# Hybrid encoder on one core: the gate z projected 512 columns at a time, and a place of its own for each final half's 1/rms

## The chip, the cores and the metric

The kernel runs on one core of a Trainium2 chip. The metric is the device time of the whole program in microseconds; smaller is better. Before the change it is 1213.37 us, the median of three runs (1212.6 to 1213.63).

The core's engines run side by side, each through its own instructions in a fixed order, and wait for each other through semaphores: TensorE (PE; its weight loads are listed as PEld), VectorE (DVE), ScalarE (ACT), GpSimd (POOL), and SyncE (SP), which here only issues transfers between HBM and the on-chip memory. Matrix products land in PSUM banks, each of 128 partitions by 512 float32.

## What is computed

Two layers of a hybrid encoder over 512 tokens of width 1024, float32, then a final RMSNorm. Cut to what matters here:

```python
for i in range(DEPTH):                                   # DEPTH = 2
    h = rms_norm(x, norm_mix_w[i])
    proj = jnp.einsum("bld,de->ble", h, w_in[i])
    q, k, v, z, xbc_raw, dt_raw = jnp.split(proj, split_at, axis=-1)   # z: 512 columns
    ...                                                  # attention on q, k, v
    ssd_out = ssd_mixer(z, xbc_raw, dt_raw, ...)         # scan in 4 chunks of 128 tokens
    x = x + jnp.einsum("ble,ed->bld", jnp.concatenate([attn_out, ssd_out], -1), w_out[i])
    x = x + ffn(rms_norm(x, norm_ffn_w[i]))              # SwiGLU
return rms_norm(x, final_norm_w)

# at the end of ssd_mixer
y = y.reshape(b, l, SSD_WIDTH) * jax.nn.silu(z)          # the gate
yg = y.reshape(b, l, SSD_GROUPS, SSD_WIDTH // SSD_GROUPS)
yg = yg * lax.rsqrt(jnp.mean(yg * yg, axis=-1, keepdims=True) + EPS)
```

## The kernel before, in words

Activations lie transposed: 8 tiles of 128 features by 512 tokens. Every float32 operand of a large product is split into a rounded high part and a low rest, and a product is three matmuls, high by high, high by low and low by high (`mm3` L417, `mm3a` L423).

**The weight stream.** All weights come in pieces of 128 by 1024 in one fixed list, `chunks` (L109 to L133): per layer k/v/dt, then what `ORDER` (L54) names (x for the convolved x/B/C columns, q and z in two halves of 256 columns of two pieces each), then eight pieces of w_out, then the FFN. SP loads a piece into one of two raw buffers (`load` L169, bufs=2). ACT casts it to the high part and DVE subtracts to the low part, 512 columns at a time (L191, L192), into one of four buffers each (WB, L31). `next` (L196) splits the piece asked for and the two after it (`AHEAD = 2`) and loads a third.

**The mixer** (L446 to L977) interleaves three generators (`drain` L892): `att` (32 heads-by-query-blocks, four per block: scores L712/L713, maximum on DVE L714, exponential on ACT L716, transposes L719, product with V L729), `fill` (the projections of `ORDER`, and after the scan the first half of the output product, `out_half` L824) and `ssd` (decay matrices L759 to L798, `chunk` L800 with L804 and L812, `finish` L917). This order of emission is a priority; a list scheduler then fixes each engine's final order. In `token_major` (L431) the stationary operand is a 128 by 128 block of tokens and the moving one a weight block of 256 columns: for one half of z, 4 token chunks of 8 row blocks of 3 matmuls (L427, L428, L429). `z_done` (L850) empties a chunk's bank: tanh and a scaled copy on ACT (L856, L857), one combining instruction on DVE (L858).

**The end.** `Last` (L361) turns the last FFN product's tiles back to token rows. The last tile comes in two halves of 256 tokens (`down` L382): each half's mean of squares becomes 1/rms by an integer guess and three Newton steps on DVE (`rsqrt` L285, twelve instructions behind L400), and two 128-row blocks are scaled by it (on ACT L407 and L410, on DVE L412) and sent out in four transfers (L413). `rsqrt` keeps its result in a place named after its argument `name` (L288), one buffer deep.

Of the kernel before, what the change touches and what calls it, by code (L numbers as in the profile page):

```python
# [15 lines left out]
F32 = mybir.dt.float32  # L16
F32R = mybir.dt.float32r
I32 = mybir.dt.int32
AF = mybir.ActivationFunctionType
# [4 lines left out]
P = 128  # L24
# [3 lines left out]
S = 512  # L28
# [25 lines left out]
ORDER = "x4 q0 x5 x7 x6 x3 x0 x1 x2 q1 z0 z1".split()  # L54
# [24 lines left out]
def tile_hybrid_encoder(ctx, tc, xt_d, par_d, rope_d, snw_d, w_kvdt, w_xbc, w_q, w_z, w_out, w_gate, w_up, w_down, out_d):  # L79
# [29 lines left out]
    for l in range(L):  # L109
# [3 lines left out]
        for what in ORDER:  # L113
            i, lo = int(what[1]), what in POOL_LO
            if what[0] == "x":
                stream(w_xbc[l, i], 1024, lo, 512)
            else:
                for j in range(2):
                    stream({"q": w_q, "z": w_z}[what[0]][l, 2 * i + j], 1024, lo, 512)
# [15 lines left out]
    class Stream:  # L135
# [40 lines left out]
        def fetch(self, j, a, b, queue=nc.sync):  # L176
            self.fetched[j] = queue.dma_start(self.raw[j][:, a:b], chunks[j][0][:, a:b])
# [183 lines left out]
    class Last(Norm):  # L361
# [20 lines left out]
        def down(self, m, cols):  # L382
# [18 lines left out]
            rt = rsqrt(nrm, mm, 2, "rfin")  # L401
# [29 lines left out]
    def token_major(ps, op, n, after=None, behind=None):  # L431

        w = W.take(2)
        for c in range(NC):
            b = ps[c] if isinstance(ps, list) else ps(c)
            for k in range(KT):
                wh, wl = (t[:, k % 4 * n:(k % 4 + 1) * n] for t in w[k // 4])
                with tc.issue_after(behind.ins) if behind and c == 0 and k > 1 else nullcontext():
                    mm3a(b[:, :n], wh, wl, op, k, c, k == 0, k == KT - 1)
            if after is not None:  # L440
                after(c, b)
            yield

    nrm0 = Norm(pc("nmix", 0, 8), xT)

    def mixer(l, norm, mx):  # L446
# [403 lines left out]
        def z_done(hf):  # L850
            def fin(c, ps):
                if hf not in gz:
                    gz[hf] = mx.tile([P, NC, 256], F32, name=f"gz{hf}", tag=("kd", "Btok")[hf])
                th = mx.tile([P, 256], F32, name="zth", tag="t3", bufs=B3)
                zs = gz[hf][:, c]
                A.activation(th, ps[:, :256], AF.Tanh, scale=rth[:, c:c + 1])  # L856
                A.activation(zs, ps[:, :256], AF.Copy, scale=rth[:, c:c + 1])  # L857
                V.scalar_tensor_tensor(zs, th, 1.0, zs, ALU.add, ALU.mult)  # L858
            return fin

        def fill():
            for what in ORDER:
                i = int(what[1])
                if what[0] == "q":
                    yield from qproj(i)
                elif what[0] == "z":
                    yield from token_major(lambda c: bank("a"), op, 256, z_done(i))
# [338 lines left out]
```

## Time and profile before

| | us |
|---|---|
| median of three runs | 1213.37 |
| the profiled execution | 1212.78 |
| its span, first to last instruction | 1211.0 |
| PE busy | 1190.3 (98%) |
| DVE busy | 902.2 (75%) |
| ACT busy | 633.3 (52%) |
| POOL busy | 149.8 (12%) |

PE is busy in nearly every slice and its granted clock stands at the top level nearly throughout. The span holds, for each of two layers, a mixer (about 20 to 260 us and 600 to 850 us) and an FFN, and at the end the output of the final norm, in which PE no longer works. Busy shares are means over these stretches: what an edit is worth is read in its own stretch.

### The profile page before, as it was taken

The page shows a single profiled execution, that of the slowest core. Times are in us where ns is not written, and L with a number is a line of the kernel's source. Part 1 is how long each engine was busy: PE and PEld are TensorE (multiplying, and loading weights), DVE is VectorE, ACT ScalarE, POOL GpSimd, SP SyncE. Part 2 cuts the span into 40 slices and gives each one's busy share as a digit, 9 for nine tenths or more (in the row PEclk, how much of TensorE's full clock was granted, in tenths as well). Part 3 has the DMA queues.
Part 4 walks back from the last instruction along what each step waited for, and adds up shares of the span by engine and source line. Part 5 has one row for each costly group of instructions (what it writes and reads, how often), then busy time and mean ns, then how long its engine had stood idle before and what let it go on. Part 6 is the DMA issues. An engine that isn't in the chain of part 4 may idle for free.

```text
span 1211.0 us, 19732 instructions
## 1 busy us (share of the span) xinstructions
PE 1190.3 (98%) x7720; PEld 1056.5 (87%) x7720; DVE 902.2 (75%) x1477; ACT 633.3 (52%) x1208; POOL 149.8 (12%) x140
## 2 busy tenths in 40 slices
PE   9999999999999999999999999999999999999996
PEld 7889887788899899899898888878879989989985
DVE  7999986568886676677779977866688857847842
ACT  5668775344444354254556876844335524533634
POOL 0202432012000000000211053401020000000011
PEclk9999999999999999999999999999999999999998
DMA  6221111225143233231433111312242432332121
GB/s 223 96 75 54 44 53 53 73 84 165 58 135 123 70 122 114 67 100 40 151 126 103 60 35 56 95 33 91 81 146 96 140 105 70 124 108 83 36 79 70
DMA packets 47534, 110.04 MB, mean 91 GB/s; under 512 B 5425, under 2 KB 5937, under 8 KB 47441
## 3 DMA queue, kind: packets, MB, share of 16 engines
q1 hardware_dynamic: 46720, 107.68, 28.0%
q8 instruction: 60, 0.98, 0.3%
q10 hardware_dynamic: 720, 1.11, 0.3%
q14 instruction: 34, 0.27, 0.1%
HBM read 104.44 MB, written 4.33 MB: 90 GB/s over the span
## 4 chain that ended last, share of the span: by engine, by line
PE 89%; DVE 5%; ACT 3%; DMA 1%; issue 1%; POOL 0%; SPq 0%; ACTq 0%; DVEq 0%; POOLq 0%
PE ps_a L1068 6%; PE ps_a L1067 6%; PE ps_a L1066 6%; PE ps_a L419 5%; PE ps_a L420 5%; PE ps_a L421 5%; PE ps_s L1112 3%; PE ps_s L1114 3%; PE ps_s L1113 3%; PE ps_a L1113 3%; PE ps_a L1112 3%; PE ps_a L1114 3%; PE ps_s L1068 3%; PE ps_s L1067 3%; PE ps_s L1066 3%; PE ps_t L729 3%
## 5 line engine op out<-in xcount | busy, mean ns | idle before, releaser
L191 ACT CAST whi<-wraw 128x512 fp32r<-128x512 f32 (+4 forms) x183 | 125.5, 714 | 211.6 <-PE ps_a L420 52.7
L191 ACT CAST whi<-sraw 128x1024 fp32r<-128x1024 f32 x126 | 131.7, 1050 | 141.0 <-DVE sraw L166 40.4
L192 DVE TENSOR_TENSOR wlo<-wraw,whi 128x512 fp32r<-128x512 f32 (+4 forms) x183 | 149.4, 831 | 54.2 <-ACT whi L191 53.1
L192 DVE TENSOR_TENSOR wlo<-sraw,whi 128x1024 fp32r<-128x1024 f32 x126 | 153.6, 1223 | 46.3 <-ACT whi L191 46.1
L328 POOL TENSOR_TENSOR ssq<-ssq,sqt 128x512 f32<-128x512 f32 x17 | 24.9, 1463 | 680.0 <-ACT sqt L325 679.3
L419 PE MATMUL ps_a<-xh,whi 128*128 128x512 f32 x272 | 107.2, 397 | 0.6 <-DVE x L834 0.3
L421 PE MATMUL ps_a<-xh,wlo 128*128 128x512 f32 x272 | 106.6, 392 | 0.0
L420 PE MATMUL ps_a<-xl,whi 128*128 128x512 f32 x272 | 106.3, 392 | 0.0
L166 DVE TENSOR_TENSOR sraw<-sraw 128x1024 f32<-128x1024 f32 x72 | 88.0, 1222 | 1.0
L1068 PE MATMUL ps_a<-ss,wlo 128*128 128x256 f32 x288 | 81.7, 284 | 0.0
L1066 PE MATMUL ps_a<-ss,whi 128*128 128x256 f32 x288 | 81.5, 283 | 0.0
L1067 PE MATMUL ps_a<-ss,whi 128*128 128x256 f32 x288 | 81.5, 283 | 0.0
L1068 PE MATMUL ps_a<-s,wlo 128*128 128x256 f32 x288 | 81.1, 283 | 0.0
L1067 PE MATMUL ps_a<-s,whi 128*128 128x256 f32 x288 | 81.1, 283 | 0.0
L1066 PE MATMUL ps_a<-s,whi 128*128 128x256 f32 x288 | 79.8, 283 | 0.0
L427 PE MATMUL ps_a<-whi,xh 128*128 128x256 f32 (+1 forms) x256 | 74.2, 291 | 0.1
L428 PE MATMUL ps_a<-wlo,xh 128*128 128x256 f32 (+1 forms) x256 | 73.9, 290 | 0.0
L429 PE MATMUL ps_a<-whi,xl 128*128 128x256 f32 (+1 forms) x256 | 71.9, 286 | 0.0
L1113 PE MATMUL ps_a<-hid,whi 128*128 128x512 f32 x176 | 68.9, 391 | 1.7 <-DVE hid L1012 1.7
L1112 PE MATMUL ps_s<-hid,whi 128*128 128x512 f32 (+1 forms) x182 | 70.0, 385 | 0.3 <-DVE a__3261 L1009 0.2
L1113 PE MATMUL ps_s<-hid,whi 128*128 128x512 f32 (+1 forms) x182 | 69.8, 384 | 0.0
L1114 PE MATMUL ps_s<-hid,wlo 128*128 128x512 f32 (+1 forms) x182 | 69.7, 383 | 0.0
(412 smaller groups left out, 3441.7 us busy)
## 6 DMA issues: line engine op xcount, KB each, us to landing
sraw<-in_w_gate SPq DMA_DIRECT2D x72, 256.0 KB, 3.3
sraw<-in_w_up SPq DMA_DIRECT2D x72, 256.0 KB, 4.0
wraw<-in_w_down SPq DMA_DIRECT2D x48, 384.0 KB, 3.2
wraw<-in_w_xbc SPq DMA_DIRECT2D x16, 512.0 KB, 3.2
wraw<-in_w_out SPq DMA_DIRECT2D x16, 512.0 KB, 3.3
wraw<-in_w_q SPq DMA_DIRECT2D x8, 512.0 KB, 3.5
wraw<-in_w_z SPq DMA_DIRECT2D x8, 512.0 KB, 3.3
wraw<-in_w_gate SPq DMA_DIRECT2D x8, 512.0 KB, 3.2
```

The source lines that it names most:

```text
L166: V.tensor_tensor(q[to], q[to], q[by], ALU.add)
L191: A.copy(hi[:, u], raw[:, u])
L192: (G if lo_pool else V).tensor_tensor(lo[:, u], raw[:, u], hi[:, u].bitcast(F32), ALU.subtract)
L419: T.matmul(ps, lhsT=wh, rhs=op.h[k], start=first, stop=False)
L420: T.matmul(ps, lhsT=wh, rhs=op.l[k], start=False, stop=False)
L421: T.matmul(ps, lhsT=wl, rhs=op.h[k], start=False, stop=last)
L1066: T.matmul(out, lhsT=wh[:, o:o + P], rhs=x_[:, 0, i], start=first and i + j == 0, stop=False, skip_group_check=True)
L1067: T.matmul(out, lhsT=wh[:, o:o + P], rhs=x_[:, 1, i], start=False, stop=False, skip_group_check=True)
L1068: T.matmul(out, lhsT=wl[:, o:o + P], rhs=x_[:, 0, i], start=False, stop=i == 3, skip_group_check=True)
L1112: T.matmul(ps[:, cols], lhsT=w1[:, o:o + P], rhs=h, start=f == a, stop=False)
L1113: T.matmul(ps[:, cols], lhsT=w1[:, o:o + P], rhs=g, start=False, stop=False)
L1114: T.matmul(ps[:, cols], lhsT=w2[:, o:o + P], rhs=h, start=False, stop=f == b - 1)
```

## The change

Two edits that have nothing to do with each other.

The final halves' 1/rms get a name each (`rfin0`, `rfin1`), so that each has its own buffer.

z is projected in one pass of 512 columns instead of two of 256. Its four weight pieces, which held four row blocks of 256 columns, now hold two row blocks of 512 columns; as the arrays in HBM are as before, each piece is loaded by two transfers, one for each half of the columns. All four pieces are needed for every token chunk, so `token_major` takes four pieces before the first chunk, and with `AHEAD = 0` it splits nothing beyond them. One bank of 512 columns is emptied by one tanh of 512 columns, two copies of 256 and two combining instructions of 256. The generator yields twice per chunk, so that its eight turns in `drain` stay.

```diff
-ORDER = "x4 q0 x5 x7 x6 x3 x0 x1 x2 q1 z0 z1".split()
+ORDER = "x4 q0 x5 x7 x6 x3 x0 x1 x2 q1 z".split()
...
         for what in ORDER:
-            i, lo = int(what[1]), what in POOL_LO
+            i, lo = int(what[1:] or 0), what in POOL_LO
             if what[0] == "x":
                 stream(w_xbc[l, i], 1024, lo, 512)
             else:
-                for j in range(2):
-                    stream({"q": w_q, "z": w_z}[what[0]][l, 2 * i + j], 1024, lo, 512)
+                for j in range(2 if what[0] == "q" else 4):
+                    if what[0] == "q":
+                        stream(w_q[l, 2 * i + j], 1024, lo, 512)
+                    else:
+                        u = slice(j % 2 * 512, j % 2 * 512 + 512)
+                        stream([w_z[l, h + j // 2][:, u] for h in (0, 2)], 1024, lo, 512)
...
         def fetch(self, j, a, b, queue=nc.sync):
-            self.fetched[j] = queue.dma_start(self.raw[j][:, a:b], chunks[j][0][:, a:b])
+            src = chunks[j][0]
+            if isinstance(src, list):
+                for i, s in enumerate(src):
+                    to = self.raw[j].rearrange("p (k i n) -> p k i n", k=2, i=2)[:, :, i]
+                    self.fetched[j] = queue.dma_start(to, s.rearrange("p (k n) -> p k n", k=2))
+                return
+            self.fetched[j] = queue.dma_start(self.raw[j][:, a:b], src[:, a:b])
...
-            rt = rsqrt(nrm, mm, 2, "rfin")
+            rt = rsqrt(nrm, mm, 2, f"rfin{i}")
...
     def token_major(ps, op, n, after=None, behind=None):
 
-        w = W.take(2)
+        per = WU // n
+        W.AHEAD = 2 if per == 4 else 0
+        w = W.take(KT // per)
+        W.AHEAD = 2
         for c in range(NC):
             b = ps[c] if isinstance(ps, list) else ps(c)
             for k in range(KT):
-                wh, wl = (t[:, k % 4 * n:(k % 4 + 1) * n] for t in w[k // 4])
+                wh, wl = (t[:, k % per * n:(k % per + 1) * n] for t in w[k // per])
...
             yield
+            if per == 2:
+                yield
...
-        def z_done(hf):
-            def fin(c, ps):
+        def z_done(c, ps):
+            th = mx.tile([P, S], F32, name="zth", tag="t3", bufs=B3)
+            A.activation(th, ps, AF.Tanh, scale=rth[:, c:c + 1])
+            for hf in range(2):
                 if hf not in gz:
                     gz[hf] = mx.tile([P, NC, 256], F32, name=f"gz{hf}", tag=("kd", "Btok")[hf])
-                th = mx.tile([P, 256], F32, name="zth", tag="t3", bufs=B3)
-                zs = gz[hf][:, c]
-                A.activation(th, ps[:, :256], AF.Tanh, scale=rth[:, c:c + 1])
-                A.activation(zs, ps[:, :256], AF.Copy, scale=rth[:, c:c + 1])
-                V.scalar_tensor_tensor(zs, th, 1.0, zs, ALU.add, ALU.mult)
-            return fin
+                zs, h = gz[hf][:, c], slice(256 * hf, 256 * hf + 256)
+                A.activation(zs, ps[:, h], AF.Copy, scale=rth[:, c:c + 1])
+                V.scalar_tensor_tensor(zs, th[:, h], 1.0, zs, ALU.add, ALU.mult)
...
-                    yield from token_major(lambda c: bank("a"), op, 256, z_done(i))
+                    yield from token_major(lambda c: bank("a"), op, S, z_done)
```

Line numbers in the orders of the changed kernel are its own: up to fifteen higher than before's for the same statement (L191 is L201, L192 is L202, L427 to L429 are L437 to L439, L712 is L727, L716 is L731, L729 is L744).

ACT, layer 0, before: the casts of the third and fourth w_out piece (`whi<-wraw`) stand between the evacuations of the last z chunks (`zth`, `gz`), behind the exponentials of heads 23 and 24.

```order
L91 COPY t_ring<-ps_t 128x512
L716 ACTIVATE p_ring,sums<-ps_s,nm 128x512
L91 COPY ee<-ps_m 128x512
L716 ACTIVATE p_ring,sums<-ps_s,nm 128x512
L191 CAST whi<-wraw 128x512 x2
L856 ACTIVATE zth<-ps_a,rth 128x256
L857 ACTIVATE gz_2053<-ps_a,rth 128x256
L191 CAST whi<-wraw 128x512 x2
L787 ACTIVATE ee<-ee 128x512
```

The first and second w_out piece were cast earlier, at heads 12 and 13. In the change all four pieces' casts stand among the exponentials (`p_ring,sums`) of heads 17 to 20:

```order
L201 CAST whi<-wraw 128x512 x2
L731 ACTIVATE p_ring,sums<-ps_s,nm 128x512 x2
L201 CAST whi<-wraw 128x512
L802 ACTIVATE ee<-ee 128x512
L201 CAST whi<-wraw 128x512
L91 COPY qr<-ps_t 128x128
L91 COPY ee<-ps_m 128x512
L91 COPY t_ring<-ps_t 128x512
L201 CAST whi<-wraw 128x512 x2
L802 ACTIVATE ee<-ee 128x512
L91 COPY t_ring<-ps_t 128x512
L731 ACTIVATE p_ring,sums<-ps_s,nm 128x512
```

The first pair of casts now stands ahead of heads 17 and 18, and the row behind the last one shown is the last pair, between heads 19 and 20.

PE, layer 0, before: the end of the z projection (`ps_a<-whi,xh` and its companions, 256 columns) lies between the scores of head 24 and its products with V.

```order
L429 MATMUL ps_a<-whi,xl_153 128x256
L427 MATMUL ps_a<-whi,xh_151 128x256
L428 MATMUL ps_a<-wlo,xh_151 128x256
L429 MATMUL ps_a<-whi,xl_153 128x256
L427 MATMUL ps_a<-whi,xh_151 128x256
L428 MATMUL ps_a<-wlo,xh_151 128x256
L429 MATMUL ps_a<-whi,xl_153 128x256
L729 MATMUL ps_t<-t_ring,Vt 64x128 x8
L674 MATMUL ps_t<-ident,qd 128x128 x4
```

In the change the last z matmuls (512 columns) stand ahead of the scores (`ps_s<-KK,qh`, `ps_s<-KK,ql`) of heads 19 and 20:

```order
L437 MATMUL ps_a<-whi,xh_151 128x512
L438 MATMUL ps_a<-wlo,xh_151 128x512
L439 MATMUL ps_a<-whi,xl_153 128x512
L437 MATMUL ps_a<-whi,xh_151 128x512
L438 MATMUL ps_a<-wlo,xh_151 128x512
L439 MATMUL ps_a<-whi,xl_153 128x512
L727 MATMUL ps_s<-KK,qh 128x512
L728 MATMUL ps_s<-KK,ql 128x512
L727 MATMUL ps_s<-KK,qh 128x512
L728 MATMUL ps_s<-KK,ql 128x512
```

z ends four heads earlier in PE's order; behind it comes no large product until the output product.

DVE, at the end, before: the last step of the first half's 1/rms, then the second half's start (`mf` its mean square, `rfini` the integer, `rfin` the result).

```order
L296 SCALAR_TENSOR_TENSOR rfin<-rfint,rfin 128x2
L400 TENSOR_SCALAR mf<-ps_m 128x2
L290 TENSOR_SCALAR rfini<-mf 128x2
L292 TENSOR_SCALAR mf<-mf 128x2
L291 TENSOR_SCALAR rfin<-rfini 128x2
L294 TENSOR_TENSOR rfint<-rfin 128x2
L295 TENSOR_TENSOR rfint<-rfint,mf 128x2
```

In the change the integer and the result of the second half have their own names, and the result's first instruction moves up by one place:

```order
L306 SCALAR_TENSOR_TENSOR rfin_12042<-rfin0t,rfin_12042 128x2
L410 TENSOR_SCALAR mf<-ps_m 128x2
L300 TENSOR_SCALAR rfin1i<-mf 128x2
L301 TENSOR_SCALAR rfin_12099<-rfin1i 128x2
L302 TENSOR_SCALAR mf<-mf 128x2
L304 TENSOR_TENSOR rfin1t<-rfin_12099 128x2
L305 TENSOR_TENSOR rfin1t<-rfin1t,mf 128x2
```

Nothing else is moved there.

## Rows read from the trace of the kernel before

**Rows 1.** Page, busy time of each engine (share of the span) and instructions.

```profile
PE 1190.3 (98%) x7720; PEld 1056.5 (87%) x7720; DVE 902.2 (75%) x1477; ACT 633.3 (52%) x1208; POOL 149.8 (12%) x140
```

**Rows 2.** Mixer stretches: us, busy PE PEld DVE ACT POOL (instructions), clock, DMA, GB/s.

```profile
111.00:146.00 35.00, 34.86 (x264) 30.14 (x263) 31.34 (x55) 23.87 (x59) 17.59 (x17) 1.00 0.14 46
146.00:181.00 35.00, 35.00 (x278) 30.73 (x277) 29.35 (x69) 26.35 (x71) 15.40 (x14) 1.00 0.19 51
181.00:201.00 20.00, 17.87 (x131) 13.22 (x130) 15.25 (x36) 12.58 (x36) 7.27 (x8) 1.00 0.30 85
700.00:740.00 40.00, 40.00 (x304) 34.91 (x302) 32.01 (x64) 27.17 (x77) 19.73 (x18) 1.00 0.18 56
740.00:780.00 40.00, 39.90 (x317) 34.81 (x316) 33.13 (x74) 29.89 (x80) 16.60 (x15) 1.00 0.23 71
780.00:797.00 17.00, 15.49 (x136) 12.21 (x134) 11.51 (x33) 12.23 (x35) 5.34 (x6) 1.00 0.10 31
```

**Rows 3.** Timeline of PE, z of layer 0: start us, us, engine, line, tile, shape.

```profile
155.84 0.28 PE L428 MATMUL ps_a<-wlo,xh 128*128 128x256 f32 x1
...
157.40 0.28 PE L429 MATMUL ps_a<-whi,xl 128*128 128x256 f32 x1
```

**Rows 4.** Timeline of PE, last FFN product, 512 columns.

```profile
1188.28 0.39 PE L1112 MATMUL ps_a<-hid,whi 128*128 128x512 f32 x1
...
1190.78 0.39 PE L1114 MATMUL ps_a<-hid,wlo 128*128 128x512 f32 x1
```

**Rows 5.** Users of the split weights: first and last start (layer 0 window; whole span).

```profile
L427 PE MATMUL ps_a<-whi,xh x96: 274/283/386, 86.3 to 175.9; 128*128 128x256 f32 x96
...
L427 PE MATMUL ps_a<-whi,xh x256: 274/283/592, 6.0 to 770.2; 128*128 128x256 f32 x112, 128*128 128x272 f32 x16
```

**Rows 6.** Chain that ended last, layer 0: start us, us, what.

```profile
119.11 1.07 DVE gz L858
...
129.47 1.04 ACT whi L191 x2
...
154.62 0.24 PE ps_s L712
```

**Rows 7.** ACT and DVE, 100 to 200 us, by form: busy us, mean ns, idle before.

```profile
L191 ACT CAST whi<-wraw 128x512 fp32r<-128x512 f32 x12 | 6.9, 633 | 0.6 <-PE ps_a L429 0.6
L856 ACT ACTIVATE zth<-ps_a,rth 128x256 f32<-128x256 f32 x8 | 3.9, 481 | 0.8 <-POOL xs L94 0.5 <-DVE gz L858 0.3
...
L192 DVE TENSOR_TENSOR wlo<-wraw,whi 128x512 fp32r<-128x512 f32 x12 | 8.0, 686 | 0.7 <-ACT whi L191 0.7
```

**Rows 8.** Transfers by line: count, KB each, median us from issue to landing.

```profile
wraw<-in_w_out SPq DMA_DIRECT2D x16, 512.0 KB, 3.3
...
wraw<-in_w_z SPq DMA_DIRECT2D x8, 512.0 KB, 3.3
```

**Rows 9.** What SP's queue waited for: us in total, times, longest us.

```profile
SPq L886 <- PE ps_m L812: 39.9, 10, 12.0
...
SPq L940 <- DVE t L94: 8.6, 2, 4.3
```

**Rows 10.** Timeline of DVE at the end.

```profile
1200.92 0.17 DVE L292 TENSOR_SCALAR mf<-mf 128x2 f32<-128x2 f32 x1
1203.59 0.17 DVE L291 TENSOR_SCALAR rfin<-rfini 128x2 int32<-128x2 int32 x1 [2.50 <-ACT o L410]
...
1205.56 1.15 DVE L412 TENSOR_SCALAR o<-o,rfin 128x512 f32<-128x512 f32 x3
```

**Rows 11.** Timeline of ACT at the end.

```profile
1202.34 1.22 ACT L410 ACTIVATE o<-o,rfin 128x512 f32<-128x512 f32 x2
1205.62 0.62 ACT L407 ACTIVATE o<-ps_t,rfin 128x128 f32<-128x128 f32 x2 [2.06 <-DVE rfin L296]
1206.13 0.72 ACT L410 ACTIVATE o<-o,rfin 128x512 f32<-128x512 f32 x1
```

**Rows 12.** Output transfers' issues: ns min/median/max, first and last start us.

```profile
L413 SPq DMA_DIRECT2D out_t<-o x8: 332/344/403, 1201.7 to 1207.5; - x8
```

**Rows 13.** Stretches of the end; the last two columns are DMA share and GB/s.

```profile
1202.60:1205.50 2.90, 0.00 (x0) 0.00 (x0) 1.60 (x10) 0.96 (x2) 0.00 (x0) 0.50 0.94 357
1205.50:1207.00 1.50, 0.00 (x0) 0.00 (x0) 1.17 (x4) 1.23 (x3) 0.00 (x0) 0.50 0.04 15
1207.00:1209.90 2.90, 0.00 (x0) 0.00 (x0) 0.00 (x0) 0.00 (x0) 0.00 (x0) 0.50 0.93 354
```

More of the change, by code (lines that the diff above doesn't have):

```diff
@@ L848, in to_mixed @@
             V.tensor_tensor(mixed.l.half(half)[:, :, c * P:(c + 1) * P], merge(tp, 4, P), hv.bitcast(F32), ALU.subtract)
-        def z_done(hf):
-            def fin(c, ps):
+        def z_done(c, ps):
+            th = mx.tile([P, S], F32, name="zth", tag="t3", bufs=B3)
+            A.activation(th, ps, AF.Tanh, scale=rth[:, c:c + 1])
+            for hf in range(2):
                 if hf not in gz:
                     gz[hf] = mx.tile([P, NC, 256], F32, name=f"gz{hf}", tag=("kd", "Btok")[hf])
-                th = mx.tile([P, 256], F32, name="zth", tag="t3", bufs=B3)
-                zs = gz[hf][:, c]
-                A.activation(th, ps[:, :256], AF.Tanh, scale=rth[:, c:c + 1])
-                A.activation(zs, ps[:, :256], AF.Copy, scale=rth[:, c:c + 1])
-                V.scalar_tensor_tensor(zs, th, 1.0, zs, ALU.add, ALU.mult)
-            return fin
+                zs, h = gz[hf][:, c], slice(256 * hf, 256 * hf + 256)
+                A.activation(zs, ps[:, h], AF.Copy, scale=rth[:, c:c + 1])
+                V.scalar_tensor_tensor(zs, th[:, h], 1.0, zs, ALU.add, ALU.mult)
         def fill():
             for what in ORDER:
-                i = int(what[1])
+                i = int(what[1:] or 0)
                 if what[0] == "q":
```

## The prediction

> **What bounds the kernel now.** I read the page first, for the busy shares: PE is at work for 98% of the span, DVE for 75%, ACT for half [rows 1]. So the first question of any edit is whether it takes work from PE. Then the stretches, because z is projected inside the mixers and a mean over the span says nothing of them. In both mixers PE is busy without a gap while z is in its queue, at the full granted clock (1.00, the 2.4 GHz level), and loses time only at the end: 2.1 us of 20 in layer 0 (181 to 201 us) and 1.5 us of 17 in layer 1 (780 to 797 us) [rows 2]. There z is over, its last matmuls starting near 175.9 and 770.2 us [rows 5], and what is left for PE is small pieces of attention and scan, each handed over by ACT or DVE. DVE is not far behind PE in these stretches: 31.3 of 35 us, then 29.4 of 35 [rows 2]; the chain that ended last runs partly over z's combining instruction and over casts of weights [rows 6]. At the very end PE is out, and the chain is a ladder of small DVE instructions, ACT scalings and output transfers [rows 10 to 13].
>
> **Edit 1, z at 512 columns: what it takes from PE.** Per layer the old z is 2 halves x 4 chunks x 8 row blocks x 3 = 192 matmuls of 256 columns, the new one 96 of 512. What counts is the distance from start to start, since the listed durations overlap. z's own: 13 steps from 155.84 to 157.40 us, 0.120 us each [rows 3]. Of 512 columns, in a closed run at the same clock: 11 steps from 1188.28 to 1190.78 us, 0.227 us each [rows 4]. Two narrow matmuls take 0.240 us and one wide 0.227: 0.0127 us less for each of 192 pairs in the program, 2.4 us. It is PE time out of stretches that PE fills, so it is worth its full size unless waits grow.
>
> The Trainium skill's page "TensorE: Matmul & The Clock Gate", section "Back-to-back issue gap", gives an isolated distance of N/2.4 + 2.5 ns: 109.2 and 215.8 ns, so that a pair would save 2.5 ns and the edit 0.5 us, a sum 1.9 us worse than mine. The rows stand against it: narrow matmuls that each load their weights lie 120 ns apart [rows 3].
>
> **Edit 1, smaller parts.** ACT gets 4 wide tanhs per layer for 8 narrow ones of 0.48 us [rows 7]. A wide tanh is not in the rows; between one narrow and two it is 0.48 to 0.96 us, so ACT gains 0 to 1.9 us a layer, off the path since PE is the full engine: I take nothing. Were ACT the bound it would help, so leaving it out costs the forecast at most that. Copies and combining instructions keep their number, and splits of weights too. z's loads are 8 transfers a layer instead of 4, of half the size; the old ones land in 3.3 us [rows 8]. A piece that lands twice as late, 3.3 us more, is the upper end; between 100 and 200 us the casts waited 0.6 us, for PE to give back a buffer and not for a transfer [rows 7], so I take nothing here either.
>
> **Edit 1, what moves.** Two things, both against the gain. First, z ends four heads earlier in PE's order, ahead of the scores of heads 19 and 20, in layer 0 near the place of the old 154.6 us [rows 6]; before, it ended near 176. So the stretch in which PE has only the small handed-over pieces gets longer. Of the 21.4 us from 154.6 to 176.0, 72 narrow matmuls took 8.6, so 12.8 us of other PE work loses its filler. If PE then idles as at the end of layer 0 now, 2.13 of 20 us, that is 1.4 us a layer, at the most 2.7 in the two. If it doesn't idle, nothing: DVE has 84% and ACT 75% there [rows 2], so there is some room, and z's matmuls that come sooner fill PE earlier. I take 1.0, a little under the middle, since four casts and four subtractions of w_out leave the earlier stretch (111 to 146 us) with the change, where DVE is at 90%.
>
> Second, that same move. Before, the split ran two pieces ahead, so the first two w_out pieces were split at heads 12 and 13. Now all four buffers hold z until its last chunk, and four pieces are split behind it: 8 casts of 0.63 and 8 subtractions of 0.69 us [rows 7], in ACT's row ahead of the exponentials of heads 17 to 20. Pieces three and four can be loaded only when pieces one and two have left the raw buffers, so ACT's row also waits for two loads of 3.3 us [rows 8]. What is queued behind those casts on ACT is the exponentials, and PE's transposes wait for them. The cover is z's last chunk on PE, 24 x 0.227 = 5.4 us, and attention's own work between. On SP the third piece's load now stands behind one transfer of the residual (L886) and that of the norm's weights (L940), which wait for buffers of the scan; L940 waited 4.3 us each time, L886 mostly for the scan's L812 [rows 9]. Both waits end with the first chunks of the scan, ahead of the burst, so I expect them to be over by then. I take nothing for it beyond the 1.0 above; its upper end is the slower rival below.
>
> **Edit 2, the final 1/rms.** Before, the second half's result has the first half's place. Its first instruction (L291) stands ready behind L292 at 1200.92 us but starts at 1203.59, after 2.50 us of waiting for ACT's last scaling of the first half [rows 10]. With its own place it goes at about 1201.1. The Newton steps then end at 1203.0 instead of 1205.5, and DVE's scalings follow at once. ACT finishes the first half at 1202.34 + 1.22 = 1203.56 [rows 11] and is late next: its second half, 1205.62 to 1206.85, starts 2.06 us sooner. By ACT and SP's issues (the last at 1207.5 [rows 12]) the end would move by 2.1 us. But the transfers are late behind them: the first half's megabyte fills the DMA engines (94%) until about 1205.4, then they stand idle (4%) until 1207.0, and the second half's fills them until about 1209.8 [rows 13]. Closing that gap is the most the transfers can give: 1207.0 - 1205.4 = 1.6 us. I take 1.6; the bounds are 1.0 (a transfer's issue and start still leave a hole) and 2.1.
>
> **Sum.** 1212.8 (the profiled execution) - 2.4 + 1.0 - 1.6 = 1209.8 us. The median of the runs is 0.6 above that execution, so 1210.4.
>
> **Rivals.**
>
> *More than PE's own saving.* In 111 to 146 us the chain runs over DVE and ACT, w_out's casts and z's combining among them [rows 6], and these leave. If waiting shrinks instead of growing, at most the 2.13 + 1.51 + 0.24 = 3.9 us that PE idles in the mixer stretches [rows 2] can go; half of it gives 1212.8 - 2.4 - 1.9 - 1.6 + 0.6 = 1207.5. For it: DVE's 90%. Against it: PE has no idle to give where they leave.
>
> *z's saving is eaten.* The longer stretch without filler idles like the old one, 2.7 us: 1212.8 - 2.4 + 2.7 - 1.6 + 0.6 = 1212.1. For it: 11% and 9% idle where z is over [rows 2]. The skill's rule on the distance would end nearly there too, at 1212.8 - 0.5 + 1.0 - 1.6 + 0.6 = 1212.3; against rows 3 and 4 I give it 1 in 50, inside this case.
>
> *Slower: the w_out pieces in one burst.* If the exponentials of heads 17 to 20 wait for the whole burst, a layer pays two loads and eight casts, 2 x 3.3 + 8 x 0.63 = 11.6 us, less the 2.5 that four casts took at this place before, less 5.4 of z's cover: 3.7, and 7.4 in two layers: 1212.8 - 2.4 + 7.4 - 1.6 + 0.6 = 1216.8. It makes the kernel slower from 2.0 us a layer on. Against it: ACT has a quarter of its time free there [rows 2], and the loads run beside other exponentials.
>
> That an edit doesn't do what it says is excluded by the orders for z and for the last normalization.
>
> **How the numbers follow.** Forecast 0.50, its own range 1208.9 to 1211.9; more than PE's saving 0.22; saving eaten 0.18; burst 0.10. A measurement of this kernel tells 0.2% from no change, 2.4 us: faster is under 1210.9, slower over 1215.8. Of the forecast two thirds lie under 1210.9: faster 0.33 + 0.22 = 0.55. The rest of it, the eaten saving and a fifth of the burst are the same: 0.17 + 0.18 + 0.02 = 0.37. Slower 0.08. The range leaves out a tenth at each side: 1206.8 to 1214.2.
>
> **What would show it.** z's matmuls 0.227 us apart and 96 a layer. L291's successor for the second half right behind the integer, with no wait for ACT; the output transfers in one closed block of some 5.4 us. PE's idle behind z's end at 1 us over before, not 3; then the wait for t_ring and p_ring names it. If ACT's casts behind z show waits for w_out's transfers, and exponentials of heads 17 to 20 late, the burst is at work. Wrong would be a PE that idles more than 2 us a layer over before, or output transfers that still stand apart.

## The result and the profile after

The change makes the kernel slower: 1219.87 us (median; 1219.63 to 1221.65) against 1213.37, a ratio of 1.0063 [1.0051, 1.0075]. The forecast was 1210.4 us, with a chance of 0.08 for slower. The execution that was profiled in that measurement was a disturbed one, left out here (2999 us; 512-column matmuls 620 ns apart where they otherwise lie 227 to 234, at a listed clock of 1.00), so the profile shown is that of a second measurement of the same kernel. Its median is 1221.65 us, beside 1212.43 for the kernel before on the same chip, ratio 1.007 [1.0056, 1.0084]; the profiled execution took 1221.35 us, with a span of 1219.6 us. "After" means this one.

The page's busy times, which answer to [rows 1]:

```profile
PE 1197.4 (98%) x7528; PEld 1045.3 (86%) x7528; DVE 904.9 (74%) x1477; ACT 632.8 (52%) x1200; POOL 148.9 (12%) x140
```

192 matmuls fewer, as worked out, and yet PE is busy 7.1 us longer. A busy PE isn't a PE at its peak: it also counts matmuls at a lower clock and ones whose start is held up. The mixer stretches, columns as in [rows 2]:

```profile
111.00:146.00 35.00, 35.00 (x240) 28.07 (x237) 26.28 (x51) 21.30 (x54) 17.85 (x17) 1.00 0.02 6
146.00:181.00 35.00, 31.88 (x204) 24.26 (x203) 32.22 (x62) 26.61 (x68) 13.79 (x13) 1.00 0.27 91
181.00:201.00 20.00, 18.48 (x140) 14.64 (x140) 16.18 (x39) 12.86 (x38) 8.06 (x8) 1.00 0.22 67
700.00:740.00 40.00, 40.00 (x261) 32.63 (x260) 29.80 (x58) 26.17 (x74) 18.75 (x17) 1.00 0.08 27
740.00:780.00 40.00, 38.13 (x234) 30.29 (x233) 34.29 (x72) 29.78 (x76) 14.89 (x15) 0.94 0.27 86
780.00:797.00 17.00, 16.78 (x118) 13.22 (x118) 11.91 (x27) 9.69 (x27) 7.09 (x8) 0.93 0.20 63
```

Three things differ from before. In 146 to 181 us PE has 3.1 us of gaps where it had none. In layer 1 the granted clock is 0.94 and 0.93 where it was 1.00. And the work has moved between the stretches: DVE gives back 5 us in 111 to 146 and has 2.9 more in 146 to 181.

To lay time side by side I take a mixer from the start of its first head's exponential to the start of the last of the sixteen additions that take the output sums out of PSUM (L834 before, L849 after).

| | before | after |
|---|---|---|
| mixer 0 | 165.3 | 167.6 |
| from there to mixer 1 (FFN 0 in it) | 422.4 | 423.9 |
| mixer 1 | 167.1 | 172.9 |
| from there to the end | 366.0 | 365.6 |

So 8.1 of the 8.6 us by which the span grew lie in the mixers, and layer 1 has most of them. The same two mixers as stretches, columns as in [rows 2], before and then after:

```profile
90.24:255.54 165.30, 162.70 (x1105) 134.91 (x1104) 126.38 (x243) 104.77 (x274) 46.75 (x43) 1.00 0.19 60
677.93:845.06 167.13, 165.26 (x1140) 139.96 (x1139) 125.94 (x245) 107.21 (x277) 49.53 (x43) 1.00 0.19 61
```

```profile
89.67:257.23 167.56, 162.27 (x1009) 129.57 (x1008) 127.77 (x242) 104.24 (x270) 46.66 (x43) 1.00 0.18 59
681.10:854.02 172.92, 170.17 (x1044) 137.49 (x1043) 127.93 (x246) 107.00 (x273) 48.59 (x43) 0.98 0.18 60
```

PE's visible idle time, length less busy time, grows by 2.7 us in mixer 0 and by 0.9 in mixer 1.

**How the time goes in layer 1.** PE in the changed kernel, start and length in us; the bracket is idle time and what ended it:

```profile
771.70 0.43 PE L744 MATMUL ps_t<-t_ring,Vt 128*64 128x128 f32 x2
773.54 0.50 PE L798 MATMUL ps_m<-segr,segl 80*128 80x512 f32 x1 [1.41 <-DVE ee L801]
774.20 1.09 PE L744 MATMUL ps_t<-t_ring,Vt 128*64 128x128 f32 x14 [0.17 <-ACT t_ring L91]
```

The next decay matrix (L798) waits for DVE to empty its bank, and PE has nothing else. DVE in the same microseconds:

```profile
768.30 2.86 DVE L809 SCALAR_TENSOR_TENSOR gg<-st,dt,gg 128x128 f32<-128x128 f32 x4 [0.52 <-POOL gg L94]
771.08 0.75 DVE L873 SCALAR_TENSOR_TENSOR gz<-zth,gz 128x256 f32<-128x256 f32 x2
771.75 1.13 DVE L809 SCALAR_TENSOR_TENSOR gg<-st,dt,gg 128x128 f32<-128x128 f32 x4
772.80 0.68 DVE L801 TENSOR_TENSOR ee<-ps_m,ee 128x512 f32<-128x512 f32 x1
```

DVE's row is fixed, and the awaited instruction (L801) stands last in it, behind both halves of a gate chunk and eight products of the scan. Before, the same row of instructions (two fours of `gg`, a `gz`, then `ee`) ran from 761.89 to 766.0, and PE had z to work on until the next decay matrix:

```profile
767.41 0.36 PE L427 MATMUL ps_a<-whi,xh 128*128 128x256 f32 x1
...
767.85 0.28 PE L427 MATMUL ps_a<-whi,xh 128*128 128x256 f32 x1
767.96 0.40 PE L783 MATMUL ps_m<-segr,segl 80*128 80x512 f32 x1
```

Here the gap is paid a second time in clock. After, columns as in [rows 2]:

```profile
770.00:775.00 5.00, 3.24 (x24) 2.07 (x24) 5.00 (x14) 4.73 (x14) 0.75 (x2) 1.00 0.00 0
775.00:780.00 5.00, 5.00 (x26) 4.74 (x24) 4.12 (x18) 3.83 (x12) 1.03 (x1) 0.54 0.22 56
780.00:785.00 5.00, 5.00 (x27) 4.28 (x25) 3.95 (x8) 1.17 (x2) 1.71 (x2) 0.77 0.34 105
```

PE is busy for 3.24 of 5 us, and behind that the granted clock is 0.54, nearly all of the stretch at the lower level (1.2 GHz), then 0.77: (0.46 + 0.23) x 5 = 3.4 us of PE lost. The scan's sixteen matmuls in that stretch, after and before:

```profile
775.96 3.51 PE L819 MATMUL ps_m<-xs,gg 128*128 128x64 f32 x16
```

```profile
772.40 1.89 PE L804 MATMUL ps_m<-xs,gg 128*128 128x64 f32 x16
```

**And in layer 0.** DVE of the changed kernel, then of the kernel before, where heads 17 and 18 get their maxima:

```profile
152.03 2.08 DVE L809 SCALAR_TENSOR_TENSOR gg<-st,dt,gg 128x128 f32<-128x128 f32 x4
154.03 0.75 DVE L873 SCALAR_TENSOR_TENSOR gz<-zth,gz 128x256 f32<-128x256 f32 x2
154.71 1.91 DVE L809 SCALAR_TENSOR_TENSOR gg<-st,dt,gg 128x128 f32<-128x128 f32 x4
156.55 1.27 DVE L729 TENSOR_REDUCE nm<-ps_s 128x1 f32<-128x512 f32 x2
```

```profile
148.58 1.27 DVE L714 TENSOR_REDUCE nm<-ps_s 128x1 f32<-128x512 f32 x2
149.78 1.06 DVE L94 TENSOR_TENSOR t<-qr,tabq 128x256 f32<-128x256 f32 x1
150.76 0.95 DVE L858 SCALAR_TENSOR_TENSOR gz<-zth,gz 128x256 f32<-128x256 f32 x1
151.64 1.13 DVE L794 SCALAR_TENSOR_TENSOR gg<-st,dt,gg 128x128 f32<-128x128 f32 x4
```

The order is turned round. z's third chunk now goes over PE ahead of these two heads, so their maxima stand behind the gate and the scan in DVE's row, and the first exponential starts at 157.26 instead of 149.61 us. z's last matmul is at 160.5 us (before 176.1) and at 757.5 (770.5): the filler is gone some 13 to 16 us sooner, and the scores of six heads (19 to 24), not of four, that stood ahead of its end now stand behind it.

In layer 0 the heads make most of this up: head 17's exponential is 8.2 us late, counted from the mixer's start, head 25's is 1.2 early (99.4 us for 100.6), and the last is 3.2 late. In layer 1 they don't: 5.8 late at head 17, 7.2 at head 25 (104.2 for 97.0), 8.5 at the last.

Layer 0 has the same gap ahead of L798 too (1.40 us, until 178.49). Its stretches after:

```profile
175.00:180.00 5.00, 3.26 (x25) 2.07 (x24) 5.00 (x14) 4.73 (x15) 0.69 (x1) 1.00 0.00 0
180.00:185.00 5.00, 5.00 (x40) 4.50 (x37) 4.79 (x18) 4.51 (x14) 1.08 (x1) 1.00 0.22 75
```

PE is busy for as little of it as at 770 to 775 us, and the clock stays at 1.00. In e3 (below) the clock falls behind this same gap of layer 0, to 0.50 from 180 to 185 us. So a gap of this kind is paid twice in some executions and not in others; what decides it was not shown.

### The profile page after: what moved, and what is told of

It is laid out like the page before. It is cut to its first block, busy times and chain, and to the rows that moved or that the text cites. A ratio compares the mean times of both kernels' runs of the same rounds, so it can differ in the third digit from the quotient of the medians.

```text
span 2997.3 us, 19361 instructions
## 1 busy us (share of the span) xinstructions
PE 2987.8 (100%) x7528; PEld 2229.4 (74%) x7528; DVE 906.9 (30%) x1477; ACT 644.8 (22%) x1200; POOL 135.1 (5%) x140
## 4 chain that ended last, share of the span: by engine, by line
PE 100%; DVE 0%; ACT 0%; issue 0%; ACTq 0%
PE ps_a L1082 6%; PE ps_a L1080 6%; PE ps_a L1081 6%; PE ps_a L429 5%; PE ps_a L430 5%; PE ps_a L431 5%; PE ps_a L1128 4%; PE ps_s L1126 4%; PE ps_a L1126 3%; PE ps_s L1128 3%; PE ps_a L1127 3%; PE ps_s L1127 3%; PE ps_t L744 3%; PE ps_s L1080 3%; PE ps_s L1081 3%; PE ps_s L1082 3%
## 5 line engine op out<-in xcount | busy, mean ns | idle before, releaser
L201 ACT CAST whi<-wraw 128x512 fp32r<-128x512 f32 (+4 forms) x183 | 125.3, 709 | 862.2 <-PE ps_a L430 259.1
L201 ACT CAST whi<-sraw 128x1024 fp32r<-128x1024 f32 x126 | 131.6, 1048 | 685.2 <-issue 218.8
L202 DVE TENSOR_TENSOR wlo<-sraw,whi 128x1024 fp32r<-128x1024 f32 x126 | 154.0, 1223 | 329.6 <-ACT whi L201 328.4
L202 DVE TENSOR_TENSOR wlo<-wraw,whi 128x512 fp32r<-128x512 f32 (+4 forms) x183 | 145.2, 810 | 270.6 <-ACT whi L201 270.5
L429 PE MATMUL ps_a<-xh,whi 128*128 128x512 f32 x272 | 226.4, 836 | 0.0
L431 PE MATMUL ps_a<-xh,wlo 128*128 128x512 f32 x272 | 225.5, 829 | 0.0
L430 PE MATMUL ps_a<-xl,whi 128*128 128x512 f32 x272 | 224.7, 827 | 0.0
L1080 PE MATMUL ps_a<-ss,whi 128*128 128x256 f32 x288 | 153.7, 534 | 0.0
L1081 PE MATMUL ps_a<-ss,whi 128*128 128x256 f32 x288 | 152.7, 530 | 0.0
L1081 PE MATMUL ps_a<-s,whi 128*128 128x256 f32 x288 | 152.1, 528 | 0.0
L1080 PE MATMUL ps_a<-s,whi 128*128 128x256 f32 x288 | 150.5, 529 | 0.0
L1128 PE MATMUL ps_a<-hid,wlo 128*128 128x512 f32 x176 | 147.4, 838 | 0.0
L1126 PE MATMUL ps_s<-hid,whi 128*128 128x512 f32 (+1 forms) x182 | 147.4, 810 | 0.0
L1127 PE MATMUL ps_s<-hid,whi 128*128 128x512 f32 (+1 forms) x182 | 147.4, 810 | 0.0
L1127 PE MATMUL ps_a<-hid,whi 128*128 128x512 f32 x176 | 144.7, 822 | 0.0
L1126 PE MATMUL ps_a<-hid,whi 128*128 128x512 f32 x176 | 144.5, 829 | 0.0
L431 PEld LDWEIGHTS ps_a<-xh,wlo 128*128 128x128 f32 x272 | 94.9, 349 | 66.3 <-issue 64.9
L429 PEld LDWEIGHTS ps_a<-xh,whi 128*128 128x128 f32 x272 | 94.4, 348 | 65.2 <-issue 62.9
L430 PEld LDWEIGHTS ps_a<-xl,whi 128*128 128x128 f32 x272 | 96.2, 354 | 59.7 <-issue 59.3
```

The lines of the kernel that those rows point to most:

```text
L201: A.copy(hi[:, u], raw[:, u])
L202: (G if lo_pool else V).tensor_tensor(lo[:, u], raw[:, u], hi[:, u].bitcast(F32), ALU.subtract)
L429: T.matmul(ps, lhsT=wh, rhs=op.h[k], start=first, stop=False)
L430: T.matmul(ps, lhsT=wh, rhs=op.l[k], start=False, stop=False)
L431: T.matmul(ps, lhsT=wl, rhs=op.h[k], start=False, stop=last)
L1080: T.matmul(out, lhsT=wh[:, o:o + P], rhs=x_[:, 0, i], start=first and i + j == 0, stop=False, skip_group_check=True)
```

## The experiments

Mixer lengths as above, us. Ratios are to the kernel before, run beside each on the same chip. Each pair of mixer lengths is that of one execution. Executions of one kernel lie up to 7 us apart (e14: 1218.76 to 1225.58), and the profiled one was 3.2 us below the median in e8 and 2.3 above it in e4, so a few tenths of a microsecond between two runs mean nothing.

| run | median | ratio [95%] | mixers 0, 1 |
|---|---|---|---|
| before (its profile) | 1213.37 | | 165.3, 167.1 |
| e1_after: the change again | 1221.65 | 1.0070 [1.0056, 1.0084] | 167.6, 172.9 |
| e2_rfin: 1/rms alone | 1212.81 | 1.0002 [0.9993, 1.0011] | 165.3, 166.7 |
| e3_z: z alone | 1219.97 | 1.0058 [1.0045, 1.0071] | 168.9, 172.0 |
| e4_narrow4: four pieces, narrow, old order | 1214.61 | 1.0018 [1.0009, 1.0027] | 166.8, 167.9 |
| e16_before_late: before, late splits | 1215.59 | 1.0028 [1.0018, 1.0038] | 166.4, 169.3 |
| e6_late_split: change, later splits | 1226.55 | 1.0121 [1.0106, 1.0136] | 170.2, 176.2 |
| e7_pool_lo: change, low parts on POOL | 1226.57 | 1.0119 [1.0104, 1.0134] | 169.2, 176.3 |
| e14_after_nolo: change without them | 1220.03 | 1.0070 [1.0052, 1.0088] | 165.9, 172.4 |
| e15_before_nolo: before without them | 1211.82 | 0.9991 [0.9982, 0.9999] | 163.9, 166.6 |
| e5_hold: z chunks 3, 4 held | 1231.61 | 1.0162 [1.0147, 1.0177] | 171.2, 180.9 |
| e8_hold3: chunk 4 held | 1225.49 | 1.0119 [1.0102, 1.0136] | 166.8, 174.4 |
| e13_hold2: chunk 3 held | 1222.91 | 1.0081 [1.0067, 1.0096] | 166.1, 177.6 |
| e9_pairs: gate by chunk pairs | 1224.10 | 1.0102 [1.0088, 1.0117] | 168.7, 175.2 |
| e10_pairs_hold: e9, chunk 4 held | 1227.13 | 1.0119 [1.0103, 1.0134] | 167.7, 179.6 |
| e12_pairs_late: e9, chunk 4 later | 1235.88 | 1.0192 [1.0175, 1.0208] | 173.6, 180.5 |
| e18_behind_scores: e9, held between heads | 1221.22 | 1.0077 [1.0064, 1.0089] | 166.4, 173.5 |
| e11_narrow_bank: change, narrow in one bank | 1231.23 | 1.0154 [1.0140, 1.0168] | 172.1, 177.6 |
| e17_narrow_pairs: e9, narrow in own banks | 1219.21 | 1.0060 [1.0046, 1.0073] | 165.6, 171.9 |

**Which edit.** The change again (no edit), and each part alone on the kernel before: e2 has the line below, e3 the rest.

```diff
-            rt = rsqrt(nrm, mm, 2, "rfin")
+            rt = rsqrt(nrm, mm, 2, f"rfin{i}")
```

> The changed kernel again, for an undisturbed profile: 1219.9 us as before, 6.5 above the kernel before. Theory A (the burst): nearly all of the loss, some 4 us a layer, stands in each mixer between heads 16 and 21, where the splits of the four w_out pieces stand on ACT and DVE ahead of the exponentials, and these pieces' loads come late. Theory B (the filler is gone): heads 16 to 21 take what they took, and the loss stands behind z's last matmul, where PE idles between the heads. In both the tail ends about 1.6 us sooner behind the last sums.

> The kernel before with the final halves' 1/rms a place each, and nothing else of the change. If the prediction's term holds: 1.6 us less, 1211.8 us. Rival: the DMA queue binds the end, and it stays within 0.3 us of 1213.4.

> The change without the 1/rms edit: z alone. If the tail's term holds and the two edits don't meet: 1221.5 us, 8.1 above the kernel before, some 4 us a layer. If the tail gained nothing: 1219.9.

Within the intervals all of the loss is z's, and the 1/rms edit gains nothing. In the tail it did what was forecast. DVE of e2, then SP's issues (start, from first to last issue) of e2 and of before:

```profile
1199.49 0.16 DVE L400 TENSOR_SCALAR mf<-ps_m 128x2 f32<-128x2 f32 x1 [3.35 <-PE ps_m L398]
...
1202.20 0.17 DVE L290 TENSOR_SCALAR rfin1i<-mf 128x2 int32<-128x2 int32 x1
1202.41 0.17 DVE L291 TENSOR_SCALAR rfin<-rfin1i 128x2 int32<-128x2 int32 x1
```

```profile
1203.20 4.47 SPq L413 DMA_DIRECT2D out_t<-o  x8
```

```profile
1201.71 6.17 SPq L413 DMA_DIRECT2D out_t<-o  x8
```

L291 follows at once, the issues take 1.7 us less, and the transfers stand in one block (in e2 the DMA engines are 95% busy or more in each microsecond from 1204 to 1209 us); from L400 to the span's end it is 11.4 us instead of 13.0. But L400 starts at 1199.49 where it stood at 1198.00: the time is lost ahead of it. PE's order is the same word for word, but the down product of the last FFN, which answers to [rows 4], reads

```profile
1189.27 0.40 PE L1113 MATMUL ps_a<-hid,whi 128*128 128x512 f32 x1
...
1192.30 0.40 PE L1114 MATMUL ps_a<-hid,wlo 128*128 128x512 f32 x1
```

13 steps of 0.233 us where they were 0.227. The median step of this product's matmuls (528 in layer 0) is 234 ns in every profile here with the 1/rms edit (fourteen) and 227 in every one without (five); the 512-column matmuls of the mixers keep 227 in both. In layer 0 the down product takes 123.0 us instead of 119.8 and the gate product 179.9 instead of 181.5: 1.6 us net. That accounts for FFN 0's 1.5 us above too. By stretches e2 has -1.1 us ahead of the first exponential, +1.8 and +1.2 in the two FFNs, -0.4 in mixer 1 and -1.6 in the tail: -0.1 in all. What the edit changes beside names is that one more small tile (128 by 2) is kept in on-chip memory; how that would act on matmuls was not tried.

**Which part of z.** e4 holds four pieces and splits w_out late like the change, but runs narrow matmuls half by half in the old order, without the 1/rms edit:

```diff
+            halves = [(lambda k, hf=hf: (w[k // 2], slice(k % 2 * 512 + hf * 256, k % 2 * 512 + hf * 256 + 256)), after(hf)) for hf in range(2)]
+        for at, done_ in halves:
+            for c in range(NC):
```

> The kernel before with the change's four z pieces (two row blocks of all columns, all four held until the second half's last matmul, no split ahead of them), but z projected 256 columns at a time, in eight narrow groups in the old order. Theory A (the pieces that are held and the w_out splits that move behind them): as slow as z alone or worse by the 2.4 us of PE that the wide matmuls save: 1221 to 1224. Theory B (z's end in PE's order): z still runs in eight groups to the same place, so 1213 to 1215.

2.3 us of mixer are there without any wide matmul; from e4 to e3 it is 6.2 more, though the wide matmuls themselves save 2.4. PE's visible idle time is only 1.1 of that; the lower clock is 5.1 (3.4 in layer 0, 1.7 in layer 1, where e4 has none).

**The late splits.** e16 splits all four early w_out pieces behind head 24 in the kernel before (its own z pieces); e6 does so in the change (e16 also keeps the second half of z from splitting ahead):

```diff
+                        if half and n == 0:
+                            for ins in heads[23]:
+                                late.enter_context(tc.issue_after(ins.ins))
                         wh, wl = W.next()
```

> The kernel before with narrow z and its own z pieces, but all eight w_out splits of the mixer's first half held behind head 24. Theory D: the whole cost of the narrow kernel on four pieces is the late splits, so 1214 to 1216. If the four pieces that are held and their two loads each cost it: 1212 to 1213.

> The change with z where it is, but all eight w_out splits held behind head 24 on ACT and DVE, where they stand with narrow matmuls on the same four pieces. Theory A (the splits ahead of the exponentials of heads 17 to 20): most of the loss goes, 1213 to 1215. Theory B: little goes, since TensorE still ends z as early; 1218 to 1221.

Late splits alone cost 3.3 us of mixer, no less than e4's 2.3, so the four held pieces show no cost beyond them. Behind head 24 DVE is full; e16's stretch 180 to 190 us, and that of before:

```profile
180.00:190.00 10.00, 8.36 (x60) 6.54 (x60) 10.00 (x15) 5.69 (x16) 5.06 (x4) 1.00 0.60 194
```

```profile
180.00:190.00 10.00, 8.66 (x62) 6.82 (x62) 7.05 (x12) 4.68 (x14) 6.06 (x6) 1.00 0.64 184
```

e6's theory A fell: later than in the change is worse still, by 4.9 us. What the splits cost where the change has them, at heads 17 to 20, no run measures by itself.

**Is it a burst on DVE and ACT?** e7 gives the low parts of these pieces to POOL, e14 leaves them out, and e15 leaves them out of the kernel before; the outputs of e14 and e15 lack that correction.

```diff
-            stream(w_out[l, 1, i], 1024, 0, 512)
+            stream(w_out[l, 1, i], 1024, 1, 512)    # e7; 2 in e14 and e15: no subtraction
```

> The change with the low halves of the four w_out pieces of the mixer's first half subtracted on POOL in place of DVE: 8 subtractions of 0.69 us a layer leave DVE. If DVE is what bounds heads 16 to 21 (it is busy in all of 165 to 170 and 175 to 180 us of the change's profile): 4 to 6 us a layer less DVE work there, and 1214 to 1217. If TensorE's order alone decides: 1219 to 1222.

> The change without the eight subtractions that make the low halves of the mixer's four first w_out pieces (the high half is multiplied in their place, so the output lacks that correction); TensorE's and ACT's work stays. It takes 8 by 0.69 us of DVE a layer out of heads 17 to 21. Theory D: at least 3 us a layer less, 1213 to 1216, and TensorE's idle time in 160 to 180 us falls from 3.1 to under 1.5. If DVE is not what binds: under 1 us a layer, 1219 to 1222.

> The same left out of the kernel before, where four of the eight stand between heads 12 and 13. Theory D: less than half of what it gives the change, 1209.5 to 1212.5. If the subtractions cost the same wherever they stand: as much as the change gains.

The theory fell. Without the subtractions the mixers are 2.2 us shorter than after (338.3 for 340.5), without them before is 1.9 shorter too (330.5 for 332.4), and the medians hardly move. On POOL a subtraction takes 1.34 us, and the kernel is slower. In e14 PE has 2.4 us of gaps in layer 0 where after has 3.1:

```profile
146.00:181.00 35.00, 32.63 (x215) 25.50 (x214) 28.04 (x58) 28.12 (x73) 13.76 (x13) 1.00 0.29 91
```

**Can z be given back its place?** The change with z's later chunks held behind named instructions, by a table of which half chunk waits for which head (e5 here):

```diff
+HOLD = {(2, 0): 17, (2, 1): 19, (3, 0): 21, (3, 1): 23}
...
+                hold = HOLD.get((c, k // 4)) if per == 2 else None
+                if hold is not None:
+                    behind = heads[hold]
```

e8 holds chunk 4 alone (heads 22 and 24), e13 chunk 3 alone (18 and 20), all three behind a head's first score matmul.

> The change, with z's third and fourth chunk held back on TensorE: their four halves of 12 matmuls may issue only behind the score matmuls of heads 18, 20, 22 and 24, which is about where the eight narrow groups of the kernel before ended. The w_out splits then stand behind head 22 by themselves. Theory B (the early end of z takes the filler and puts two heads behind z's third chunk): the loss goes but for what the split of four pieces in a row cost with narrow matmuls (2.2 us), less the 2.4 us of the wide matmuls: 1212 to 1214. Theory A (the splits that are late and bunched): no gain, 1219 to 1221.

> The change with only z's fourth chunk held back (12 matmuls behind head 22, 12 behind head 24); the third stays ahead of heads 17 and 18. If the filler behind head 18 is the cause: as with both held, 1212 to 1215. If the third chunk ahead of heads 17 and 18 is the cause (their exponentials come 8 us later than before in layer 0): 1217 to 1220.

> The change with only z's third chunk held (12 matmuls behind head 18's scores, 12 behind head 20's); the fourth follows by itself, mostly ahead of head 22. Theory D (before 150 us TensorE is full and DVE is not, behind it DVE is full, and what TensorE does too early there costs as much DVE work later): the heads from 16 on come earlier as in the run with both held, and z's end is not late: 1214 to 1218. Theory B as first put (two heads behind the third chunk): the same. If any hold is bad because TensorE then waits in order for a chain that is not ready (it idled 2.8 us at 151 us with both held): 1222 to 1232.

None gains: e5 and e8 are slower than the change, e13 can't be told from it (its interval overlaps that of e1), and none shortens mixer 1. In e5 the gaps in layer 0 grow and the clock falls there too:

```profile
146.00:181.00 35.00, 30.41 (x185) 23.90 (x185) 26.01 (x55) 22.41 (x58) 11.94 (x12) 0.91 0.18 54
```

Such a hold can put 12 z matmuls between the two score matmuls of a head (heads 17 and 18 in e5), and the late gate goes with a late end of the scan: its last piece comes 128.3 us into mixer 1 in e5, 122.3 after. e9 to e18 go on from there. e9 keeps the gate by pairs of chunks, so that the first two need not wait for a buffer (`Btok`) that the scan still holds:

```diff
+            i = c // 2
+            if i not in gz:
+                gz[i] = mx.tile([P, 2, S], F32, name=f"gz{i}", tag=("kd", "Btok")[i])
```

e10 and e12 are e9 with chunk 4 held (heads 18 and 20; 22 and 24); e18 holds chunk 3 behind both score matmuls of head 18 and chunk 4 behind the last transposes of heads 19 and 21.

> The change, with z's gate kept by pairs of chunks in place of column halves: chunks 0 and 1 in the buffer that is free early, chunks 2 and 3 in the one that waits for the states. No bank then waits for the states before the third chunk, whose 24 matmuls move ahead of head 13 to 14; the fourth stays behind head 18. Theory P (the pacing: the first chunk's bank is held until the states are done at 140 us, its gate's copies fall into the stretch in which DVE is full, and the third chunk stands ahead of heads 17 and 18): most of the loss goes, 1212 to 1216. Theory F (TensorE lacks the filler behind head 18, whatever stands ahead): 1218 to 1223, since z still ends as early.

> The same by pairs, with the fourth chunk cut in two: 12 matmuls behind head 18's scores, 12 behind head 20's. Theory F: better than by pairs alone, by 1 to 3 us. Theory P: within 1 us of it.

> By pairs, with the fourth chunk's halves behind the scores of heads 22 and 24, where the last two narrow groups of the kernel before stood. Theory F: the best of the three, 1211 to 1213. Theory P: as by pairs alone, or 1 to 2 us worse, since the gate of the last chunk is then done later and the scan's finish waits for it.

> Wide z by pairs of chunks with TensorE's order of the narrow kernels: the third chunk behind both score matmuls of head 18, the fourth in halves behind the transposes of heads 19 and 21; DVE then takes the maximum of heads 17 and 18 ahead of the scan's products, as in the kernel before. Theory U: the heads lose nothing, the late splits cost their 2 to 3 us and the wide matmuls save up to 2.4: 1211 to 1215. If wide units cost wherever they stand: 1220 to 1228.

Theories P and F both fell. Freeing the buffer gains nothing: e9 is slower than the change. Giving it a later end of z doesn't help: e10 is no better than e9, and e12, which was to be the best, is the slowest of all. e18 undoes the turn of layer 0 (head 17 comes 58.5 us into the mixer, before 59.4, after 67.6) and brings the end of the heads there back to within 0.3 us of before, but the scan's last piece comes at 118.5 us for 112.7 before and 117.0 after, and e18's interval overlaps that of the change. So undoing the turn of heads 17 and 18 does not bring the time back.

**Width, or the unit that is handed over?** e11 runs each chunk of the change as 48 narrow matmuls into the two halves of one bank; e17 is e9 with narrow matmuls and a bank for each 256 columns.

```diff
+            for u, k in ((u, k) for u in range(0, n, 256) for k in range(KT)):      # e11
...
+                    mm3a(b[:, u:u + 256], wh, wl, op, k, c, k == 0, k == KT - 1)
```

```diff
+        for c, u in ((c, u) for c in range(NC) for u in range(0, n, 256)):          # e17
...
+                    mm3a(b[:, :256], wh, wl, op, k, c, k == 0, k == KT - 1)
```

> The change with each chunk's 24 wide matmuls as 48 narrow ones into the two halves of the same bank; what leaves the bank, when, and into which buffers is as in the change. Theory P: the loss stays and the 2.4 us of TensorE come back on top, 1221 to 1224. If the wide matmuls themselves were the cause (a bank that is filled by longer instructions, heads that wait behind them): near the narrow kernel on the same four pieces, 1214 to 1216. Theory F: TensorE has the work of the kernel before again, 48 by 0.12 us a chunk, so 1214 to 1218.

> The change's four pieces and chunk-by-chunk order, the gate by pairs of chunks, but narrow matmuls, and a bank and an evacuation for every 256 columns. Theory U (the unit of 512 columns in a bank is what lets z run ahead of the heads): as the narrow kernel on the same pieces, 1213 to 1216. If the order of the columns is what costs: 1224 to 1231, as with narrow matmuls into shared banks.

The width of a matmul isn't it: narrow ones in units of 512 columns (e11) make the third slowest kernel of all, slower than either theory had it. Against e9, which has the same pieces, chunk order and gate, e17's smaller units take 6.4 us off the mixers, though its matmuls cost 2.4 more. So theory U holds for the unit's size, but not for the whole: e17 ends between its two forecasts. From 740 to 780 us it has little idle time and the full clock, where after had 1.87 us and 0.94:

```profile
740.00:780.00 40.00, 39.31 (x298) 33.39 (x297) 34.91 (x76) 30.00 (x79) 17.37 (x16) 1.00 0.27 80
```

Yet its mixer 1 is 4.8 us over before. What is late there is attention: the reciprocal of the heads' sums comes 120.7 us into the mixer in e17, 122.4 after and 114.0 before. The scan's last transposed half is copied out at 117.0 in e17, 122.3 after and 119.2 before. The heads fall behind late: head 22's exponential comes 83.2 us into the mixer (before 83.4), head 25's 105.8 (before 97.0). Between them DVE is busy for 22.9 of 23 us (762 to 785 us), and the low part of the queries (`ql`) that head 25's scores need stands behind four products at the scan's end (`xs`) and six of eight w_out subtractions:

```profile
775.79 2.68 DVE L946 SCALAR_TENSOR_TENSOR xs<-xs,yri,snw 128x256 f32<-128x256 f32 x4
...
780.19 0.68 DVE L692 TENSOR_TENSOR ql<-ps_t,qh 128x512 fp32r<-128x512 f32 x1
```

Before, `ql` starts at 769.27 us, ahead of all of these (91.3 us into the mixer for e17's 100.8). No complete version here beat the kernel before.

## Why the prediction was wrong

- **PE's saving (-2.4): right.** Wide z matmuls lie 0.227 us apart, 8 steps here, 96 a layer:

```profile
148.46 0.39 PE L437 MATMUL ps_a<-whi,xh 128*128 128x512 f32 x1
...
150.28 0.39 PE L439 MATMUL ps_a<-whi,xl 128*128 128x512 f32 x1
```

  The condition on it failed: it was to be worth its full size "unless waits grow". They grew.
- **PE idling where z was filler (+1.0): the step that failed.** I took the rate of idling from the end of layer 0, a mean over a stretch [rows 2], as if z only filled holes of a known size, and bounded it at 2.7. What the mixers show in its place: 3.6 us more of visible idle time (2.7 in layer 0, 0.9 in layer 1), 3.4 us of lower clock behind a gap in layer 1, which my sum had nowhere, and, as +8.1 less these and less the -2.4, another 3.5 us in which PE counts as busy at the full clock but takes longer for the same work. My sign of being wrong, over 2 us a layer of idle time, is there in layer 0 alone. Two things were not in my step: units of 512 columns turn round the order of heads, gate and scan in DVE's fixed row, and a gap can take the clock with it. The rows of 768 to 775 us show both; e9 and e17 show that the size of the unit counts.
- **The moved splits (0): mis-sized.** e16 and e4 measure 3.3 and 2.3 us, for splits behind head 24 of narrow kernels. I named z's last chunk as their cover; behind it, from 160 to 185 us after, DVE is busy for 22.7 of 25 us.
- **The tail (-1.6): right where I looked.** -1.6 from L400 on. The edit's other effect, 3.0 us more in the two FFNs, can be read from no order of instructions. It outweighs the tail's gain, and only 1.5 us gained elsewhere in that execution bring e2 to 1.0002.
- **The slower rival: the direction, not the mechanism.** The exponentials of heads 17 and 18 are late as it says, but they wait for DVE's maxima (the rows of layer 0), not for the casts. Its burst would show ACT waiting for w_out's transfers; after, ACT's casts between 100 and 200 us waited 2.5 us in all, 1.5 of it for a transfer. e14, without the subtractions of that burst, is as slow.
- **By sum:** mixers +8.1, made of about -2.4 (width), +2.3 to +3.3 (late splits), and 7 to 8 for order, unit and clock. That last part is a remainder, not a measurement. Not settled is how it divides, and why layer 1 loses 4.9 us or more with every wide z: e17 mends its clock and its scan, and its heads are still 6.6 us late, with PE idle for 2.7 us of the mixer as after (before 1.9).

## What to carry to other kernels

An off-path product in a full engine is also the filler that covers hand-overs between the others: making its units larger, or ending it sooner, has to be costed by what each engine's fixed row then puts first, not by the engine's mean idle share. Where PE has a gap, look at the granted clock of the stretch behind it before pricing the gap by its length, and in more than one place: here the same gap took the clock with it in one layer and not in the other. Measure an edit to one place against the whole span: here a gain of 1.6 us at the end met 3.0 us more in matmuls that nobody had touched.

## What the runs showed of the hardware

Same matmuls in the same order, with one more small tile in on-chip memory (e2): the 512-column matmuls of the down product lie 234 ns apart for 227, those of the mixers stay at 227, and the 256-column ones of the gate product come a little closer (179.9 for 181.5 us in 1512). The cause is open.

DVE's products with two operands in the on-chip memory run slower beside POOL. After, four of `gg` took 2.86 us from 768.30, and four more 1.13 us from 771.75, when POOL had ended. POOL's row:

```profile
767.23 2.04 POOL L94 TENSOR_TENSOR gg<-st,dt 128x512 f32<-128x512 f32 x2
769.23 1.52 POOL L94 TENSOR_TENSOR xs<-xs,gz 128x256 f32<-128x256 f32 x2
```

DVE's 512-column instructions that read PSUM kept their 0.68 to 0.69 us beside POOL (764.5 to 765.8 us). The Trainium skill's page "SBUF — State Buffer", section "SBUF: two separate sides", says that a DVE instruction with two inputs in SBUF and a GpSimd one that reads SBUF shut each other out for a whole instruction; these rows agree. Before pays part of this too (1.70 and 1.62 us for its two fours at 761.89 and 763.85), so it explains 0.7 us here, not the loss.
